# The first load of a repeat-RMSNorm kernel in two parts of 16 and 112 partitions, and gamma in one transfer

## Chip, cores and metric

The kernel runs on one core of a Trainium2 chip. The metric is device time in microseconds (us). The time of the kernel before is the median of three runs, 238.63 us (238.59 to 238.70). The profile is of one further execution, which took 238.68 us; its recorded span is 236.73 us.

## What is computed

Every row of x (8 x 512 rows of 2,048 floats) is divided by its root mean square and multiplied by gamma, and every row appears twice, one after the other, in the output of 8 x 1,024 rows.

```python
def reference(x, gamma):
    x_rep = np.repeat(x, 2, axis=1)
    rms = np.sqrt((x_rep ** 2).mean(axis=-1, keepdims=True) + 1e-6)
    return ((x_rep / rms) * gamma[None, None, :]).astype(np.float32)
```

33.5 MB are read and 67.1 MB are written, all in 32-bit floats.

## The kernel before

The 4,096 rows are cut into four tiles of 1,024 rows. In a tile each of the 128 partitions holds eight neighbouring rows: 8 x 2,048 floats, 65,536 bytes, which lie in one piece in DRAM. One load (`load`, L49 and L50) is one transfer of such a tile, 8.4 MB. Each tile becomes two stores (`store`, L52 to L55): each takes four of the eight rows per partition, every one twice, so again 65,536 bytes per partition and 8.4 MB. There are four loads and eight stores, all issued by SP on one queue.

SBUF holds one tile `y` (L46) with 24 row slots per partition, used as three regions of eight slots: `first`, `second` and `third`. The function `four` (L89) does two input tiles and is called twice (L128, L129). It loads tile n across the end of `first` and the start of `second`, and tile n + 1 into `third`, and then works in place. `squares` (L57) has ACT square each row and sum it (L63), and then take the root of the means (L67). `scale` (L70) has DVE take the reciprocal (L73) and multiply each row by it and by gamma (L75), into every second slot. `repeat` (L80, L82) copies these rows into the slots between, on ACT or on DVE. Then the store of that half tile is issued.

The order on each engine is the order of the program text (`manual_schedule`, L84). On SP that is: load 0, load 1, four stores, load 2, load 3, four stores. A transfer that waits for compute, or for a region to come free, holds up the ones behind it on SP. The loads of the second call wait for stores of the first, whose regions they use again.

`constants` (L116) is run in the first call of `four`, after load 0 is issued in the text and before load 1. Its parts lie on other engines than SP: ACT issues two transfers of 4,096 bytes, the two halves of gamma, into partition 0 (L117 to L121); POOL copies that row to all partitions (L122); DVE sets the small constant (L123); and ACT takes a root of it (L126), with which the table for the square root is loaded. The second call (L129) has no constants. Gamma on all partitions is read by every multiplication of L75. The first square of L63 waits for load 0, and so do the first multiplication of L75 and the first store.

Of the kernel before, what the change touches and what calls it, by code (L numbers as in the profile page):

```python
# [1 line left out]

# [4 lines left out]


@with_exitstack
def kernel(  # L10
    ctx: ExitStack,
    tc: tile.TileContext,
    x: bass.AP,
    gamma: bass.AP,
    out: bass.AP,
):
    nc = tc.nc
    P = nc.NUM_PARTITIONS
    f32 = mybir.dt.float32
    Act = mybir.ActivationFunctionType  # L20
    Alu = mybir.AluOpType

    B, S, D = x.shape
    Bo, So, Do = out.shape
    R = So // S
    assert R == 2 and D == Do and B == Bo and So == S * R
    eps = 1e-6
    inv_d = 1.0 / float(D)


    K = 4
    N = B * S
    ntiles = N // (P * K)
    assert N % (P * K) == 0 and ntiles == 8
    H = 2
    x_t = x.rearrange("b s d -> (b s) d").rearrange("(n p k) d -> n p k d", p=P, k=H * K)
    out_t = out.rearrange("b s d -> (b s) d").rearrange("(n p h j) d -> n h p (j d)", p=P, h=H, j=K * R)

    singles = ctx.enter_context(tc.tile_pool(name="singles", bufs=1))
    rows = ctx.enter_context(tc.tile_pool(name="rows", bufs=1))  # L40
    junk = ctx.enter_context(tc.tile_pool(name="junk", bufs=1, space=bass.MemoryType.PSUM))
    small = ctx.enter_context(tc.tile_pool(name="small", bufs=4))

    y = rows.tile([P, 3 * K * R, D], f32, name="y")  # L46
    first, second, third = 0, K * R, 2 * K * R

    def load(n, at):  # L49
        nc.sync.dma_start(out=y[:, at : at + H * K, :], in_=x_t[n])  # L50

    def store(n, h, to):  # L52
        nc.sync.dma_start(
            out=out_t[n, h], in_=y[:, to : to + K * R, :].rearrange("p j d -> p (j d)")
        )  # L55

    def squares(at, rows):  # L57

        n = len(rows)
        ss = small.tile([P, n], f32, name=f"ss{n}")  # L60
        for c, k in enumerate(rows):
            sq = junk.tile([P, D], f32, name="sq")
            nc.scalar.activation(  # L63
                out=sq[:], in_=y[:, at + k, :], func=Act.Square, accum_out=ss[:, c : c + 1]
            )
        rms = small.tile([P, n], f32, name=f"rms{n}")
        nc.scalar.activation(out=rms[:], in_=ss[:], func=Act.Sqrt, scale=inv_d, bias=eps_t[:])  # L67
        return rms

    def scale(at, to, rows, rms):  # L70
        n = len(rows)
        rstd = small.tile([P, n], f32, name=f"rstd{n}")
        nc.vector.reciprocal(out=rstd[:], in_=rms[:])  # L73
        for c, k in enumerate(rows):
            nc.vector.scalar_tensor_tensor(  # L75
                out=y[:, to + R * k, :], in0=y[:, at + k, :], scalar=rstd[:, c : c + 1],
                in1=gamma_b[:], op0=Alu.mult, op1=Alu.mult,
            )

    def repeat(to, k0, k1, copy):  # L80
        y_r = y[:, to + R * k0 : to + R * k1, :].rearrange("p (k r) d -> p k r d", r=R)
        copy(out=y_r[:, :, 1, :], in_=y_r[:, :, 0, :])  # L82

    ctx.enter_context(tc.manual_schedule())  # L84

    half = K // 2
    up, down = list(range(K)), list(range(K - 1, -1, -1))

    def four(n, constants):  # L89


        load(n, first + K)
        constants()
        load(n + 1, third)
        for rows in (up[:half], up[half:]):
            scale(first + K, first, rows, squares(first + K, rows))
        repeat(first, 0, half, nc.scalar.copy)
        repeat(first, half, K, nc.vector.tensor_copy)
        store(n, 0, first)
        scale(second, second, down, squares(second, down))  # L100
        repeat(second, half, K, nc.scalar.copy)
        repeat(second, 0, half, nc.vector.tensor_copy)
        store(n, 1, second)
        roots = [squares(third + h * K, up) for h in range(H)]
        scale(third, first, up, roots[0])
        repeat(first, 0, half, nc.scalar.copy)
        repeat(first, half, K, nc.scalar.copy)
        store(n + 1, 0, first)
        scale(third + K, third, up, roots[1])
        repeat(third, 0, K, nc.scalar.copy)  # L110
        store(n + 1, 1, third)

    gamma_b = singles.tile([P, D], f32, name="gamma_b")
    eps_t = singles.tile([P, 1], f32, name="eps_t")

    def constants():  # L116
        for c0 in (0, D // 2):  # L117
            nc.scalar.dma_start(
                out=gamma_b[0:1, c0 : c0 + D // 2],
                in_=gamma[c0 : c0 + D // 2].partition_broadcast(1),  # L120
            )  # L121
        nc.gpsimd.partition_broadcast(out_ap=gamma_b[:], in_ap=gamma_b[0:1, :])  # L122
        nc.vector.memset(eps_t, eps)  # L123

        root = singles.tile([P, 1], f32, name="root")
        nc.scalar.activation(out=root[:], in_=eps_t[:], func=Act.Sqrt)  # L126

    four(0, constants)  # L128
    four(2, lambda: None)  # L129


# [1 line left out]
_INS = ['x', 'gamma']  # L133
_OUTS = [((8, 1024, 2048), 'float32')]


# [23 lines left out]
```

## Time and profile before

| what | value |
|---|---|
| median of three runs | 238.63 us |
| profiled execution, its own time | 238.68 us |
| its span | 236.73 us |
| DVE busy | 84.4 us, 36% |
| ACT busy | 110.2 us, 47% |
| POOL busy | 2.5 us, 1% |
| squares, L63, ACT | 32 of 1,878 ns |
| multiplications, L75, DVE | 32 of 2,349 ns |
| copies, L82 | 10 on ACT, mean 4,283 ns; 4 on DVE, mean 2,293 ns |
| loads, from issue to landing | 21.9 to 40.7 us, median 39.2 |
| stores, from issue to landing | 22.1 to 32.3 us, median 24.8 |
| ACT idle before L63, for a load | 71.3 us in two stretches, the longer 51.7 |
| packets of the two gamma transfers | 4 in all, on a queue of their own |

Busy time is that of the engines that compute; an issue of a transfer isn't counted in it. SP only issues transfers. The share of DMA is the mean over the 16 DMA engines of the core. The time from issue to landing holds the time in which a transfer waits in the queue behind earlier ones.

### The profile page before, as it was taken

To read this page: it belongs to the slowest core of one execution; us is meant where nothing else is said; L and a number is where in the kernel's file an instruction comes from. 1 tells how busy PE (TensorE), PEld (TensorE's weight loads), DVE (VectorE), ACT (ScalarE), POOL (GpSimd) and SP (SyncE) were. 2 spreads that over 40 slices of the span, in tenths; PEclk is the share of its full clock that TensorE was granted. 3 is DMA by queue.
4 is the path that set the end of the run, shared out by engine and by line. 5 is a ranking of instruction groups with operands and counts; after the bars stand their busy time and mean duration, and the time that the engine had idled before them with its cause. 6 is when DMAs were issued, how large, how long until landed. Compare 5 with 4: busy or idle time off the path is not lost.

```text
span 236.7 us, 218 instructions
## 1 busy us (share of the span) xinstructions
DVE 84.4 (36%) x47; ACT 110.2 (47%) x86; POOL 2.5 (1%) x5
## 2 busy tenths in 40 slices
DVE  0000495594699400000000008929909992000000
ACT  2001989479998460000000058991999947300000
POOL 0210000000000000000000000000000000000000
DMA  9898989999898989899898989899898989899894
GB/s 355 355 532 354 532 354 487 399 443 443 365 520 354 532 354 509 377 465 421 354 532 354 532 354 520 367 399 487 354 532 354 520 365 509 376 465 421 365 520 177
DMA packets 1733, 100.68 MB, mean 425 GB/s; under 512 B 194, under 2 KB 194, under 8 KB 196
## 3 DMA queue, kind: packets, MB, share of 16 engines
q1 hardware_dynamic: 1728, 100.66, 98.5%
q10 hardware_dynamic: 4, 0.01, 0.0%
q14 instruction: 1, 0.01, 0.0%
HBM read 33.56 MB, written 67.11 MB: 425 GB/s over the span
## 4 chain that ended last, share of the span: by engine, by line
DMA 45%; ACT 26%; DVE 13%; issue 1%; DVEq 0%; SPq 0%
DMA y<-in_x_dram 26%; DMA out_dram<-y 20%; ACT sq L63 15%; DVE y L75 13%; ACT y L82 11%; ACT rms L67 1%; DVE rstd L73 0%; DVEq L75 0%; SPq L50 0%
## 5 line engine op out<-in xcount | busy, mean ns | idle before, releaser
L63 ACT ACTIVATE sq<-y 128x2048 f32<-128x2048 f32 x32 | 60.1, 1878 | 72.0 <-DMA y<-in_x_dram 71.3
L75 DVE SCALAR_TENSOR_TENSOR y<-y,rstd,gamma_b 128x2048 f32<-128x2048 f32 x32 | 73.8, 2349 | 2.1 <-DMA out_dram<-y 1.5
L82 ACT COPY y<-y 128x4096 f32<-128x4096 f32 (+1 forms) x10 | 42.6, 4283 | 19.5 <-DVE y L75 19.5
L73 DVE RECIPROCAL rstd<-rms 128x4 f32<-128x4 f32 (+1 forms) x10 | 1.7, 170 | 109.0 <-ACT rms L67 109.0
L82 DVE COPY y<-y 128x4096 f32<-128x4096 f32 x4 | 9.2, 2293 | 0.1
L63 ACT ACTIVATION_READ_ACCUMULATOR sq<-y 128x1 f32 x32 | 6.0, 186 | 0.0
L67 ACT ACTIVATE rms<-ss,eps_t 128x4 f32<-128x4 f32 (+1 forms) x10 | 3.0, 297 | 0.3
L122 POOL PARTITION_BROADCAST gamma_b<-gamma_b x1 | 2.3, 2294 | 10.2 <-DMA gamma_b<-in_gamma_dram 10.2
L126 ACT ACT_TABLE_LOAD x1 | 1.3, 1283 | 1.5 <-PEq L144 1.5
L123 DVE MEMSET eps_t<- 128x1 f32 x1 | 0.1, 59 | 0.8 <-PEq L144 0.8
L126 ACT ACTIVATE root<-eps_t 128x1 f32<-128x1 f32 x1 | 0.2, 203 | 0.0
L144 POOL MEMSET const-bfloat16-1.0<- 128x1 bf16 x1 | 0.1, 103 | 0.0
L144 POOL MEMSET const-float32-0.0<- 128x1 f32 x1 | 0.1, 100 | 0.2 <-issue 0.2
L144 POOL MEMSET const-uint8-127<- 128x1 uint8 x1 | 0.1, 102 | 0.0
L144 POOL MEMSET const-float32-1.0<- 128x1 f32 x1 | 0.1, 99 | 0.0
## 6 DMA issues: line engine op xcount, KB each, us to landing
out_dram<-y SPq DMA_DIRECT2D x8, 24.8
y<-in_x_dram SPq DMA_DIRECT2D x4, 39.2
gamma_b<-in_gamma_dram ACTq DMA_DIRECT2D x2, 4.0 KB
```

The lines of the kernel that those rows point to most:

```text
L63: nc.scalar.activation(out=sq[:], in_=y[:, at + k, :], func=Act.Square, accum_out=ss[:, c : c + 1])
L67: nc.scalar.activation(out=rms[:], in_=ss[:], func=Act.Sqrt, scale=inv_d, bias=eps_t[:])
L73: nc.vector.reciprocal(out=rstd[:], in_=rms[:])
L75: nc.vector.scalar_tensor_tensor(out=y[:, to + R * k, :], in0=y[:, at + k, :], scalar=rstd[:, c : c + 1], in1=gamma_b[:], op0=Alu.mult, op ...
L82: copy(out=y_r[:, :, 1, :], in_=y_r[:, :, 0, :])
L122: nc.gpsimd.partition_broadcast(out_ap=gamma_b[:], in_ap=gamma_b[0:1, :])
L123: nc.vector.memset(eps_t, eps)
L126: nc.scalar.activation(out=root[:], in_=eps_t[:], func=Act.Sqrt)
L144: nc = _bacc.Bacc("TRN2", target_bir_lowering=False, num_devices=1)
```

## The change

Load 0 is issued as two transfers: one of partitions 0 to 15, and one of partitions 16 to 127. The other three loads stay whole. Gamma comes in one transfer of 8,192 bytes in place of two halves. The number of transfers in the program stays 14. On ACT, DVE and POOL the order and number of computing instructions are as before; the first square on ACT waits for both parts of load 0.

```diff
+    LEAD = 16
...
-    def load(n, at):
-        nc.sync.dma_start(out=y[:, at : at + H * K, :], in_=x_t[n])
+    def load(n, at, p0=0, p1=P):
+        nc.sync.dma_start(out=y[p0:p1, at : at + H * K, :], in_=x_t[n, p0:p1])
...
-        load(n, first + K)
+        if n == 0:
+
+            load(n, first + K, 0, LEAD)
+            load(n, first + K, LEAD, P)
+        else:
+            load(n, first + K)
         constants()
         load(n + 1, third)
...
     def constants():
-        for c0 in (0, D // 2):
-            nc.scalar.dma_start(
-                out=gamma_b[0:1, c0 : c0 + D // 2],
-                in_=gamma[c0 : c0 + D // 2].partition_broadcast(1),
-            )
+        nc.scalar.dma_start(out=gamma_b[0:1, :], in_=gamma.partition_broadcast(1))
         nc.gpsimd.partition_broadcast(out_ap=gamma_b[:], in_ap=gamma_b[0:1, :])
```

## The prediction

> **What bounds the kernel now.** I read the page's slices and queue table first, then the transfer view of the first 6 us, the timeline, and last the chain of waits.
>
> ```profile
> span 236.7 us, 218 instructions
> ...
> DMA  9898989999898989899898989899898989899894
> GB/s 355 355 532 354 532 354 487 399 443 443 365 520 354 532 354 509 377 465 421 354 532 354 532 354 520 367 399 487 354 532 354 520 365 509 376 465 421 365 520 177
> ...
> q1 hardware_dynamic: 1728, 100.66, 98.5%
> ...
> HBM read 33.56 MB, written 67.11 MB: 425 GB/s over the span
> ```
>
> Columns of the queue line: packets, MB, share of the 16 DMA engines' span. The 16 engines are busy 98.5% of the span; there is no idle slice, and the mean is 425 GB/s. The trace's transfer records split the 1,728 packets into 1,536 of 65,536 bytes (one partition's eight rows of x, or of the output) and 192 of four bytes (one per engine and transfer, when it is done). So each engine carries 96 large packets, 8 per transfer in 12 transfers. The median large packet took 2.418 us, and the four-byte packets that end one transfer and the next lie 19.318 to 19.326 us apart: 8 x 2.414 and some 7 ns. 96 x 2.414 = 231.7 us of the 236.73 us span. The rest is the start (first packet at 1.73 us), a slow first packet per engine (2.4 to 3.4 us), some 0.5 to 0.7 us at 115.7 to 119 us where loads follow stores, and 1.3 us from the last packet's end (235.46) to the span's end.
>
> ```profile
> DMA  0000000000099090900900000000000999990000
> GB/s 0 0 0 0 0 0 0 0 0 0 27 2621 3058 0 437 0 437 0 0 437 0 0 0 0 0 0 0 0 0 0 0 1311 2621 1311 874 874 0 0 0 0
> ```
>
> This is 0 to 6 us in slices of 0.15 us; a packet's bytes are put where it starts. 2621 GB/s over 0.15 us is six packets, 3058 is seven, 437 is one: thirteen engines start by 1.95 us, the others at 2.18, 2.53 and 2.91 us. The second sixteen start from 4.7 us on.
>
> ```profile
> 0.72 0.76 ACTq L118 DMA_DIRECT2D gamma_b<-in_gamma_dram  x2
> 0.72 0.86 SPq L50 DMA_DIRECT2D y<-in_x_dram  x2
> ...
> 1.51 1.28 ACT L126 ACT_TABLE_LOAD   x1 [1.51 <-PEq L144]
> ...
> 10.59 2.29 POOL L122 PARTITION_BROADCAST gamma_b<-gamma_b  x1 [10.16 <-DMA gamma_b<-in_gamma_dram]
> 22.61 1.88 ACT L63 ACTIVATE sq<-y 128x2048 f32<-128x2048 f32 x1 [19.61 <-DMA y<-in_x_dram]
> ...
> 27.27 4.62 DVE L75 SCALAR_TENSOR_TENSOR y<-y,rstd,gamma_b 128x2048 f32<-128x2048 f32 x2
> ...
> 39.15 0.35 SPq L53 DMA_DIRECT2D out_dram<-y  x1
> ```
>
> Columns: start, duration, engine, line, operation. The first load's rows have landed at 22.61 us, its squares start, and the first store is issued at 39.15, while the second load's last packets run until 40.9 to 41.6. Gamma's copies land by 10.59; its first reader starts at 27.27.
>
> ```profile
> 0.72 21.87 DMA y<-in_x_dram
> ...
> 76.05 23.85 DMA out_dram<-y
> ...
> 99.98 38.68 DMA y<-in_x_dram
> ...
> 196.54 7.02 ACT y L82
> ```
>
> The chain of waits puts 26% on ACT and 13% on DVE, and ends with a copy at 196.54. It stops there because no instruction follows the last store; the 33 us after it are transfers. The stretches of ACT and DVE in it lie beside a full queue; the 38.68 us of the load at 99.98 are twice 19.3, since it waits behind a store. So the bound is packets per engine, without a gap: whatever lengthens one engine's packets moves the end one for one, and compute has room.
>
> **The change part by part.** The sum is made against the profiled execution, 238.68 us (span 236.73, 1.95 outside it); the median of the three runs is 238.63, 0.05 less.
>
> *Issues.* SP issues three loads in place of two at the start (0.34 to 0.43 us each). The second load's issue moves from 1.16 to about 1.54, and it is needed only when the first one's packets end (21.6): 20 us of cover. If that cover were gone it would cost 0.38. The stores behind it wait for compute until 39.15 anyway. Sixteen more four-byte packets, one per engine: 7 ns by the spacing above.
>
> *Gamma.* One issue on ACT in place of two (512 and 213 ns). The table load at 1.51 may come 0.2 to 0.5 earlier, ahead of an ACT that idles from 3.0 to 22.6: nothing. Before, its 4,096-byte packets took 0.156 and 0.159 us on one engine, the second only at 7.50 behind two large ones; one of 8,192 bytes takes the same 0.31. POOL's broadcast (2.29) moves from 10.59 to perhaps 3, or stays; even 14 us late it would be ready for 27.27.
>
> *Waits.* The first square on ACT, the first DVE multiply and the first store wait for both parts of the load; the part of 112 decides. One or two more semaphore steps (17 to 50 ns in the trace) lie ahead of the store at 39.15, which has about 1.8 us of queue behind it (to 41). If the load itself gets longer, the second load behind it ends later by as much, so this margin stays for the engine that is last. Engines that finish early may run dry before the store; they do not set the end.
>
> *Start.* With one packet per engine to describe, the first packet may start sooner. Bound: SP's issue ends at 1.11 and the first packet starts at 1.73, so 0 to -0.62; nothing shows that the number of packets sets this, I take 0.
>
> *The lead of 16 partitions.* It has 1 MiB: 16 packets, one per engine. [...] Not shown is whether sixteen neighbouring partitions can take sixteen packets at once. Lower end: they can, 2.418 us, +0. Upper end: one after another, 16 x 2.418 = 38.7, +36.3. Far apart; the geometric middle is four packets one after another, 4 x 2.418 = 9.67 us, **+7.25**, and I take it. It would be +0 too if only a few engines carried the lead while the others went on with the 112.
>
> [...]
>
> *The 112 partitions.* Seven packets per engine: 7 x 2.418 = 16.9 us unshared, +0. [...] Paired all the time: 33.9 us, +16.9; every step as bad as the lead: 7 x 9.67 = 67.7, +50.8. It is nearest to the 128-partition row (seven eighths of it), so I stay near the lower end and take the geometric middle of unshared and paired, 16.9 x 1.414 = 23.9, **+7.0**. The later load, on the engines that are ahead, may clash with those that are behind; I count that in this term.
>
> Sum: 238.68 + 7.25 + 7.0 = **252.9 us**.
>
> **The rivals.**
>
> (1) *Lead only.* The 112 run clean. For: they are nearly the whole width. Against: their split over the engines is new. 238.68 + 7.25 = 245.9.
>
> (2) *No sharing: not slower.* The sixteen engines write the lead at full rate, as they do at every moment of before; the count of large packets per engine stays 96. Decided at the first packet: if it ends about 3 us after its start as now, this is it. Price: 7 ns more and 0 to 0.62 less, so 238.1 to 238.7; 238.6 most likely. What else moves it is an instruction fetch: at 152.64 a packet of 8,192 bytes (0.309 us) on another queue held up one engine, which ended at 235.46 against 235.04 for the next. On another engine it could give 0.4 back, or not. For: nothing in before limits an engine but its own 27.1 GB/s. Against: that rate is the same for all engines in all 1,500 packets, and whole-width transfers alone cannot tell whether it belongs to the engine or to the place that is written.
>
> (3) *Every step shared.* If the 112 are dealt in turn, sixteen neighbours are written at each step: 9.67 + 67.7 = 77.4 in place of 19.3, so 296.7. Against: the whole load, dealt so, would be as slow, and isn't.
>
> (4) *Little sharing,* two packets one after another in the lead: +2.4, 241.1.
>
> **How the numbers follow.** Forecast (both terms) 0.46, with its own range of 248.3 (one packet of the seven paired, +2.4) to 258.0 (five paired, +12.1); lead only 0.26 (to 1 us about 245.9); no sharing 0.18; every step 0.06; little sharing 0.04. A measurement of this kernel can tell about 0.2% (0.5 us) from no change. Of the 0.18, 0.04 fall below 238.15, 0.13 within, 0.01 above. Slower: 0.46 + 0.26 + 0.06 + 0.04 + 0.01 = 0.83. Range: without every step (0.06) the top is 258.0; dropping no sharing as well would leave out over 0.2, so the low end takes it in, 238.2. That leaves out 0.06, about 0.04 at the bottom and some 0.05 of the forecast's upper tail.
>
> **What would show it.** In the changed profile: first packets of some 10 us instead of 3, so in the window of the first 6 us sixteen packets start and no second sixteen; then packets of 2.4 to 4.8 us until the load lands at about 22.6 + 14 = 37 us (30 if lead only, 22.6 if no sharing); from there the old spacing of 19.32 per transfer, every later time moved alike, and the first store some 16.5 us after the landing. Gamma's broadcast stays before the first multiply. I am wrong if the first packets stay at 3 us, if time goes missing later than the first two loads, or if the queue has idle slices.

## The result and the profile after

The changed kernel takes 261.14 us (median of five runs, 260.88 to 261.62) against 238.59 us for the kernel before on the same chip (five runs, 238.51 to 238.70). The ratio is 1.0946, with a 95% interval of 1.0935 to 1.0958: it is slower by 22.5 us, and 3.1 us above the top of the predicted range. The profiled execution has a span of 259.53 us, 22.8 more than before.

First the head of the page of the changed kernel: span, the busy share of the DMA engines and the rate in 40 slices of 6.5 us, and the DMA queue of SP (packets, MB, share).

```profile
span 259.5 us, 218 instructions
...
DMA  9879988979799799799799999898999899899794
GB/s 163 162 162 323 283 202 303 485 343 465 343 485 465 343 485 465 343 485 465 343 485 394 404 475 444 374 476 384 434 475 465 364 465 475 354 465 485 343 465 182
...
q1 hardware_dynamic: 1744, 100.66, 98.0%
```

Compare the row of the DMA engines' busy share (DMA, in tenths) with the row of the rate (GB/s). The engines count as busy all along, 98.0% against 98.5% before, and yet in the first seven slices (45 us) they move 162 to 323 GB/s, and in the later ones, but for the last, 343 to 485. Busy time alone doesn't show this loss: the packets are in flight all the time, only each takes longer.

The transfer view of the first 6 us (slices of 0.15 us, as it was shown of before):

```profile
DMA  0000000000199900990000000000000000000000
GB/s 0 0 0 0 0 0 0 0 0 0 55 1748 2621 1748 0 0 437 437 0 0 0 0 0 0 0 0 0 0 0 0 0 0 0 0 0 0 0 0 0 0
```

Sixteen packets start, between 1.74 and 2.61 us, and then none: before, the second sixteen had started by 5.4 us. Both rows count a packet in the slice in which it starts, so a 0 says that no packet started there, not that the engines stood still: by the transfer records these sixteen ran until 9.3 to 11.4 us. The timeline (start, duration, engine, line, operation) has what follows:

```profile
0.73 1.39 SPq L51 DMA_DIRECT2D y<-in_x_dram  x3
...
2.62 2.29 POOL L124 PARTITION_BROADCAST gamma_b<-gamma_b  x1 [2.19 <-DMA gamma_b<-in_gamma_dram]
44.56 1.88 ACT L64 ACTIVATE sq<-y 128x2048 f32<-128x2048 f32 x1 [41.78 <-DMA y<-in_x_dram]
...
61.08 0.37 SPq L54 DMA_DIRECT2D out_dram<-y  x1
```

Load 0 lands for the first square at 44.56 us (before 22.61), and the first store is issued at 61.08 (before 39.15): 16.5 us behind the landing in both. Everything after the first load is moved by 22 us and else as it was. Gamma's broadcast starts at 2.62 us in place of 10.59, and nothing gains by it.

The trace's transfer records give the packets of load 0. A round is here sixteen packets, one per engine. The medians of the eight rounds in us:

| | 1 | 2 | 3 | 4 | 5 | 6 | 7 | 8 | sum |
|---|---|---|---|---|---|---|---|---|---|
| before | 3.04 | 2.42 | 2.42 | 2.42 | 2.42 | 2.42 | 2.42 | 2.42 | 20.0 |
| after: lead, then the 112 | 8.73 | 5.41 | 4.74 | 2.90 | 3.74 | 4.48 | 4.61 | 4.41 | 39.0 |

The median engine loses 19.0 us here. Two engines lose some 2 us more: in the fourth round, where the others' packets took 2.8 to 3.2 us, theirs took 4.6 and 4.7, and their last ones took 4.8 against 4.3 to 4.7. The last four-byte packet of load 0 is at 43.52 us against 22.23 before, 21.3 us later, and the last packet of the kernel ends at 258.22 us against 235.47, 22.75 us later. Of the 1.5 us between these two, 0.4 appear in load 1, whose first packets took 2.8 to 3.4 us, and the rest where load 2 follows stores; why it appears there is open.

### The profile page after: what moved, and what is told of

It is laid out like the page before. It is cut to its first block, busy times and chain, and to the rows that moved or that the text cites. A ratio compares the mean times of both kernels' runs of the same rounds, so it can differ in the third digit from the quotient of the medians.

```text
span 259.5 us, 218 instructions
## 1 busy us (share of the span) xinstructions
DVE 84.4 (33%) x47; ACT 110.2 (42%) x86; POOL 2.5 (1%) x5
## 4 chain that ended last, share of the span: by engine, by line
DMA 50%; ACT 24%; DVE 12%; issue 1%; SPq 0%; DVEq 0%; ACTq 0%
DMA y<-in_x_dram 32%; DMA out_dram<-y 18%; ACT sq L64 14%; DVE y L76 12%; ACT y L83 10%; ACT rms L68 0%; DVE rstd L74 0%; SPq L51 0%; DVEq L76 0%; ACTq L64 0%
```

## The experiments

Eight kernels were run. The theory at the outset ("place"): packets slow each other when the sixteen engines write partitions that lie close together or otherwise share something in SBUF. Its rivals: "source" (reading neighbouring blocks of DRAM at one time is slow), "shape" (any transfer that hasn't 128 partitions is slow), and that the two transfers as such, or gamma, are dear.

**Gamma alone.** The kernel before, with the edit of gamma only:

```diff
-        for c0 in (0, D // 2):
-            nc.scalar.dma_start(
...
+        nc.scalar.dma_start(out=gamma_b[0:1, :], in_=gamma.partition_broadcast(1))
```

> The kernel before with gamma in one transfer, load 0 whole. Every theory that puts the loss on the split load: no change, 238.3 to 238.9 us, with POOL's broadcast of gamma starting at about 2.6 us as in the changed kernel. If gamma's transfer were the cause: some 261 us.

Measured: 238.80 us against 238.74, ratio 1.000 (0.9991 to 1.0009). The broadcast of gamma comes 8 us sooner and the first square, which waits for load 0, does not:

```profile
2.62 2.29 POOL L118 PARTITION_BROADCAST gamma_b<-gamma_b  x1 [2.19 <-DMA gamma_b<-in_gamma_dram]
22.53 1.88 ACT L63 ACTIVATE sq<-y 128x2048 f32<-128x2048 f32 x1 [19.77 <-DMA y<-in_x_dram]
```

Gamma's part of the change is worth nothing.

**The split alone.** The changed kernel with gamma in two halves, so that only the split of load 0 is left of the change.

> The changed kernel with gamma in two halves again. If the split of load 0 is the whole cause: 261 us (260.5 to 261.8), the first sixteen packets taking 8 to 9.3 us as in the changed kernel. If the loss needs the gamma packet on a lead engine: back near 238.6.

Measured: 261.12 us (one run). The whole loss is that of the split load. Gamma's second half now arrives late, its broadcast starts at 12.96 us, and the first multiplication doesn't need it before 48.

**Two halves of 64 partitions.**

```diff
-    LEAD = 16
+    LEAD = 64
```

> Load 0 in two halves of 64 partitions, gamma in one transfer. Place theory (packets that go to partitions close together slow each other; the lead's 8.7 us against 2.42 is 3.6 times): in each half sixteen engines share half of the width, so a packet takes about twice 2.42, the load 8 x 4.84 = 38.7 in place of 19.3, in all about 258 us. Source theory (sixteen packets that read neighbouring 64 KB blocks of DRAM at one time slow each other): engines read blocks four apart, as far as in the whole load if each engine takes neighbours, so about 239 us. Shape theory (any transfer that hasn't 128 partitions is slow, like the 112 at 30 us in place of 16.9, 1.8 times): 8 x 2.42 x 1.8 = 34.8, about 254 us.

Measured: 260.76 us (one run), above the 258 of the place theory and far from the 239 of the source theory. The records show why it is more: after the first round, packets take 4.92 to 5.14 us, not 4.84, and the medians of the eight rounds of load 0 add up to 40.4 us in place of the 20.0 before. Shape isn't excluded by this run, which missed all three numbers.

**The same first load split by rows, not by partitions.** Both transfers have all 128 partitions: one row of 8 KB of each, then seven.

```diff
-        nc.sync.dma_start(out=y[p0:p1, at : at + H * K, :], in_=x_t[n, p0:p1])
+        nc.sync.dma_start(out=y[:, at + k0 : at + k1, :], in_=x_t[n, :, k0:k1])
...
-            load(n, first + K, 0, LEAD)
-            load(n, first + K, LEAD, P)
+            load(n, first + K, 0, 1)
+            load(n, first + K, 1, H * K)
```

> Load 0 in two transfers again, but both over all 128 partitions: the first of the eight rows of each partition, then the other seven; gamma in one transfer. Place and shape theory: every transfer has the whole width, so no loss: 238.3 to 239.2 us. Source theory: packets of 8 and 56 KB from the same spacing as the whole load, also no loss. If two transfers in place of one are dear as such: clearly slower, towards 261.

Measured: 239.42 us, ratio 1.0035 (1.0022 to 1.0047). Two transfers in place of one are not what costs 22 us. It is 0.2 us over what I expected. Load 0's last packet is no later than before (22.20 us), load 1's is by 1.0 us, with packets of 3.3 to 3.9 us near 38.6; why these are slow was not pursued.

**Loads by themselves.** This kernel computes no norm and stores only two pieces at the end; each load waits until the one before has landed and DVE has marked the tile. The lines that load (blocks are the 64 KB pieces of x, one per partition):

```
L42  y[:]         <- blocks[0:128]          L54  y[64:80]    <- blocks[192:208]
L44  y[:]         <- blocks[128:256]        L56  y[0:32]     <- blocks[224:256]
L46  y[0:16]      <- blocks[0:16]           L58  y[0:64]     <- blocks[256:320]
L48  y[0:16]      <- blocks[0:512:32]       L60  y[16:128]   <- blocks[320:432]
L50  y[0:128:8]   <- blocks[128:144]        L62  y[0:112]    <- blocks[384:496]
L52  y[0:112:7]   <- blocks[160:176]        L64, L66: one row, seven rows of all
```

> Only loads, one after another, each alone on the queue (DVE marks the tile between them); no norm is computed and only two small stores are made, so its time is not to be compared. Per packet of 64 KB: whole load of 128 partitions 2.42 us (all theories), about 21.9 us from issue to landing. Sixteen partitions 0 to 15 from sixteen neighbouring blocks of DRAM: 8 to 9.3 us as in the changed kernel. The same partitions from blocks 2 MB apart: place theory 8 to 10 us again; source theory near 2.5 to 3. Partitions 0, 8, ... 120 or 0, 7, ... 105 from neighbouring blocks: place theory 2.4 to 5 us; source theory 8 to 9.3. Partitions 64 to 79: as 0 to 15 by place and source theory. 32 partitions: place theory about half of the lead's slowing, some 10 us for two packets per engine. 64 partitions: place theory 19 to 20 us for four packets, source theory about 10. 112 partitions, 16 to 127 and 0 to 111: between 17 (no slowing when alone) and 30 us (slow by itself); shape theory 30 for both. One row of 8 KB per partition over 128 partitions: about 4 us; seven rows: 17 to 19.

The timeline of the marks (L39): the idle time in brackets is DVE's wait for the load that was issued just before it, in the order of the lines above, from L42 to L62.

```profile
23.02 0.07 DVE L39 MEMSET y<- 128x8 f32 x1 [22.14 <-DMA y<-in_x_dram]
45.07 0.07 DVE L39 MEMSET y<- 128x8 f32 x1 [21.99 <-DMA y<-in_x_dram]
56.90 0.07 DVE L39 MEMSET y<- 128x8 f32 x1 [11.77 <-DMA y<-in_x_dram]
69.12 0.07 DVE L39 MEMSET y<- 128x8 f32 x1 [12.15 <-DMA y<-in_x_dram]
76.86 0.07 DVE L39 MEMSET y<- 128x8 f32 x1 [7.67 <-DMA y<-in_x_dram]
84.28 0.07 DVE L39 MEMSET y<- 128x8 f32 x1 [7.36 <-DMA y<-in_x_dram]
96.13 0.07 DVE L39 MEMSET y<- 128x8 f32 x1 [11.79 <-DMA y<-in_x_dram]
108.51 0.07 DVE L39 MEMSET y<- 128x8 f32 x1 [12.31 <-DMA y<-in_x_dram]
131.55 0.07 DVE L39 MEMSET y<- 128x8 f32 x1 [22.98 <-DMA y<-in_x_dram]
166.00 0.07 DVE L39 MEMSET y<- 128x8 f32 x1 [34.39 <-DMA y<-in_x_dram]
198.89 0.07 DVE L39 MEMSET y<- 128x8 f32 x1 [32.83 <-DMA y<-in_x_dram]
```

The third and fourth waits are one and the same load of partitions 0 to 15, from neighbouring blocks (11.77 us) and from blocks 2 MB apart (12.15); their packets take 8.1 to 9.3 and 7.7 to 9.2 us. So it isn't the source. Sixteen partitions spread out (7.67 and 7.36 us) are faster than sixteen neighbours with the same bytes, so it isn't the number of partitions. 32 neighbours take hardly longer than 16 (12.31), and 64 take 22.98, as long as all 128 (22.14). Partitions 64 to 79 take 11.79, like 0 to 15. And the 112 partitions take 34.39 us (16 to 127) and 32.83 us (0 to 111) alone: seven packets per engine, longer than the eight of the whole load, and longer than the 30 that I had put as the upper end. Their seven rounds have medians of 4.3, 4.8, 3.5, 3.9, 4.4, 4.8 and 4.5 us in the one, and of 4.6, 4.8, 4.8, 3.3, 3.3, 4.6 and 4.8 in the other. So the slow 112 of the changed kernel need no lead ahead of them. One thing remained open: the set seven apart was expected between 2.4 and 5 us per packet, and none of its packets came near 2.4; all took 3.8 to 5.2.

**Places.** Only small transfers, without a norm, each once. Six of them have the same form and the same kind of source and differ in the first partition alone (L42 to L52).

```
L42  y[32:96:4]    L48  y[20:84:4]     L54  y[11:117:7]   L60  y[0:4]      L66  y[0:128:64]
L44  y[36:100:4]   L50  y[48:112:4]    L56  y[0:1]        L62  y[0:8:4]    L68 to L72  stores of
L46  y[40:104:4]   L52  y[0:64:4]      L58  y[0:2]        L64  y[0:64:32]  0:16, 32:96:4, 40:104:4
```

> Only small transfers, each alone; no norm is computed, and only three pieces of the output are stored, so its time is not to be compared. Sixteen partitions four apart, with the same sixteen neighbouring packets of DRAM each, and only the first partition moved: 32 to 92, 36 to 96, 40 to 100, 20 to 80, 48 to 108, 0 to 60. Source and shape theory: all of these alike, since source and shape are the same. Place theory: they differ; the fastest takes some 3 us per packet (2.42 and the 0.6 of a first packet), the slowest as long as 32 or 64 neighbours did, 4.6 to 5.1. [...] Stores of 0 to 15: 10 us per packet as in the earlier run; of 32 to 92 four apart: about 3.

The waits of the marks, again in the order of the lines, L42 to L72:

```profile
23.25 0.07 DVE L39 MEMSET y<- 128x8 f32 x1 [5.32 <-DMA y<-in_x_dram]
30.32 0.07 DVE L39 MEMSET y<- 128x8 f32 x1 [7.01 <-DMA y<-in_x_dram]
37.74 0.07 DVE L39 MEMSET y<- 128x8 f32 x1 [7.35 <-DMA y<-in_x_dram]
45.20 0.07 DVE L39 MEMSET y<- 128x8 f32 x1 [7.40 <-DMA y<-in_x_dram]
52.90 0.07 DVE L39 MEMSET y<- 128x8 f32 x1 [7.64 <-DMA y<-in_x_dram]
60.45 0.07 DVE L39 MEMSET y<- 128x8 f32 x1 [7.48 <-DMA y<-in_x_dram]
65.59 0.07 DVE L39 MEMSET y<- 128x8 f32 x1 [5.08 <-DMA y<-in_x_dram]
70.29 0.07 DVE L39 MEMSET y<- 128x8 f32 x1 [4.63 <-DMA y<-in_x_dram]
76.70 0.07 DVE L39 MEMSET y<- 128x8 f32 x1 [6.35 <-DMA y<-in_x_dram]
87.81 0.07 DVE L39 MEMSET y<- 128x8 f32 x1 [11.04 <-DMA y<-in_x_dram]
92.97 0.07 DVE L39 MEMSET y<- 128x8 f32 x1 [5.11 <-DMA y<-in_x_dram]
99.82 0.07 DVE L39 MEMSET y<- 128x8 f32 x1 [6.78 <-DMA y<-in_x_dram]
104.94 0.07 DVE L39 MEMSET y<- 128x8 f32 x1 [5.06 <-DMA y<-in_x_dram]
116.68 0.07 DVE L39 MEMSET y<- 128x8 f32 x1 [11.68 <-DMA out_dram<-y]
121.07 0.07 DVE L39 MEMSET y<- 128x8 f32 x1 [4.32 <-DMA out_dram<-y]
127.91 0.07 DVE L39 MEMSET y<- 128x8 f32 x1 [6.77 <-DMA out_dram<-y]
```

The first six alone settle it. Partitions 32 to 92 land after 5.32 us, and moving the set by four partitions makes that 7.01; moving it by eight 7.35, and then it hardly grows. The set seven apart that begins at partition 11 takes 5.08. Shape and source are the same in the six, so only the place is left. The sets of two say which partitions slow each other: 0 and 1, and 0 and 32, are slow (6.35 and 6.78 us), 0 and 4, and 0 and 64, are nearly as fast as one partition (5.11 and 5.06 against 4.63), and four neighbours take 11.04. In packets, partition 0 alone took 3.3 us, 0 and 1 took 4.2 to 4.4, and 0 to 3 took 7.7 to 8.7. Other sets of two were not tried.

The transfer records show the packets one by one. Beside each set of sixteen stands how many of its partitions are new, that is, not in the first set (32, 36, ... 92):

| set | new | packets, us |
|---|---|---|
| load, 32 to 92 | 0 | 2.4 to 3.1 |
| load, 36 to 96 | 1 | two of 4.1, the others 2.5 to 3.2 |
| load, 40 to 100 | 2 | all 4.2 to 5.2 |
| load, 20 to 80 | 3 | all 4.4 to 5.2 |
| load, 48 to 108 | 4 | all 3.9 to 4.9 |
| load, 0 to 60 | 8 | all 4.2 to 5.1 |
| store, 32 to 92 | 0 | 2.45 |
| store, 40 to 100 | 2 | four of 4.7, twelve of 2.5 |
| store, 0 to 15 | 16 | 9.8 to 10.2 |

So in the sets four apart two of a load's sixteen packets are slow with one new partition (4.1 us), and all sixteen from two on (3.9 to 5.2); in a store with two only four are (4.7). The number alone decides nothing: of the set seven apart from 11 thirteen are new, and it landed after 5.08 us. How the 112 partitions are dealt to the engines stands in no trace, and no more does it for the 128 of a whole load, whose packets took 2.42 us. In each of the four short rounds of the two 112 loads (third and fourth of the one, fourth and fifth of the other) exactly two packets are long: 4.8 and 4.9, then 4.4 and 4.6 us in the one, 4.8 and 4.8, then 4.3 and 4.5 in the other, where the remaining fourteen took 2.9 to 3.9. In the changed kernel, too, exactly two packets are long in the fourth and fifth rounds of load 0, 4.6 and 4.7, then 4.4 and 4.4 us; the first two are those of the engines that come last. That looks like the set with one new partition, only that the fourteen are slower than its 2.5 to 3.2, which isn't explained. In the other five rounds of the changed kernel's 112 all sixteen packets took 4.1 to 6.0 us, like the sets with two and more. It is no more than a likeness: which partitions meet in a round was not shown.

**The cost inside the whole kernel.** The kernel with gamma in one transfer and load 0 whole gets an extra load of 0.5 MB ahead of it, which nobody uses: half packets for sixteen neighbours, or for sixteen partitions four apart.

```diff
+        if n == 0:
+            nc.sync.dma_start(out=y[0:16, first : first + K, :], in_=x_t[3, 0:16, 0:K])
         load(n, first + K)
```

> The kernel before with gamma in one transfer, load 0 whole, and ahead of it one more load that nobody uses: half a packet (32 KB) to each of the partitions 0 to 15. If the lead costs what it does because of where it writes, in the whole kernel as alone: half of 8.7 us, so 4.4 more: 242.6 to 243.6. If a short transfer at the head is what costs, this and the next kernel are alike.

> The same with the 16 half packets going to partitions 32, 36, ... 92. Place theory: 32 KB on each engine at 2.42 us for 64 KB, 1.2 more: 239.7 to 240.4. Source and shape theory: as e5, 242.6 to 243.6.

Measured: near 242.83 us, ratio 1.0176 (1.0161 to 1.0191); far, with `y[32:96:4]` there, 240.59 us, 1.0081 (1.0065 to 1.0098). The issues of the two (kernels near, then far; last number: us from issue to landing):

```profile
y<-in_x_dram SPq DMA_DIRECT2D x1, 512.0 KB, 7.4
```

```profile
y<-in_x_dram SPq DMA_DIRECT2D x1, 512.0 KB, 3.8
```

The same bytes in the same form cost 4.1 us near and 1.85 far over the kernel before, whose runs beside them had a median of 238.74. The near one is as expected, the far one 0.2 us above the expected range; its packets themselves took 1.3 to 2.1 us. The place theory holds in the whole kernel, and source and shape fall.

No run points to a version faster than the kernel before. That kernel has the 16 engines busy for 98.5% of its span, at the whole-width rate of 2.418 us a packet, the fastest steady rate that any 64 KB packet had here.

## Why the prediction was wrong

**What bounds the kernel** was read rightly: the engines' packets. A loss in the first load went through to the end, and compute and the waits on semaphores hid nothing of it: the first store still follows the landing by 16.5 us. One of the signs of being wrong did show in small: 1.1 us went missing later than the first two loads, and no run tells why.

**Issues, gamma, waits, start**: each at nothing, and nothing it was. Gamma alone gave a ratio of 1.000. The three loads were issued within 1.39 us from 0.73. The first packets start from 1.74 to 2.61 us in place of 1.73 to 2.91: a smaller first transfer starts no sooner. That engines which are ahead may run dry before the first store without setting the end, came true for fourteen of them: their load 1 ended between 60.8 and 61.5 us, and their first store packets start from 61.9 on.

**The lead**: put at 9.67 us and +7.25. Its packets took 8.73 us in the median. The second round starts at 10.67 us in the median, against 4.93 before, so it cost +5.7. That sixteen neighbours are slowed was right, and the size 1.5 too large: 0.9 because a packet took 8.73 and not 9.67, and 0.6 because I compared it with a steady packet of 2.418, where a first one takes 3.04 anyway. That it came so near was partly luck: four packets one after another was the middle between two far ends, not read from a row. The same 1 MiB by itself took 9.40 us from its first packet's start to its last one's end, 112 GB/s.

**The 112 partitions** are the step that failed: "It is nearest to the 128-partition row (seven eighths of it), so I stay near the lower end and take the geometric middle of unshared and paired, 16.9 x 1.414 = 23.9, +7.0." Measured were 30.3 us in the median engine (the sum of its seven rounds) against 16.9, +13.4: five rounds of 4.4 to 5.4 us (+11.6) and the other two at 2.9 and 3.7 (+1.8). The last two engines lost some 2.2 more. With the 1.5 us after load 0, 5.7 + 13.4 + 2.2 + 1.5 makes 22.8, the difference of the two spans. The row was chosen by the number of partitions, but that number says nothing about it: 16 partitions took 5.3 us or 7.4 us by the place of the first one alone. No run shows the pairing of two engines from which the +7.0 was taken; in its place the records show five rounds of seven in which all sixteen packets were slow, and two in which two took 4.4 to 4.7 us and the rest 2.8 to 3.8. And in the set with two new partitions not four packets were slow but all sixteen (4.2 to 5.2 us), which no row of before could have shown. The case that I wrote down as an end, all seven paired, gave +16.9 and 262.8 us, and is nearer to the measured 261.1 than the value that I took. My range closed at "five paired", +12.1, which left out that the other two rounds lengthen too, the engines that come last, and the 1.5 us after load 0. The clash with the later load, which the prediction counted in this term, was there and small: the 0.4 us in load 1.

**The rivals.** Lead only (245.9) fell, since the 112 are slow alone. No sharing (238.6) fell at the first packet, where it was to be decided: 8.7 us, not 3, so that an engine's 27.1 GB/s (65,536 bytes in 2.418 us) became 7.5. Little sharing (241.1) fell with the lead's 8.7 us, which is more than two packets one after another. Every step as bad as the lead (296.7) fell too: the rounds of the 112 took 2.9 to 5.4 us, not 9.67. The other signs given in advance were right: no second sixteen within 6 us, the later times moved alike; the first square was to start at 37 us, and started at 44.6.

## What to carry to other kernels

Where DMA is the bound, leave a load whole over the 128 partitions; to cut it, cut along the rows of each partition, which cost 0.35% here (one row, then seven) where the cut by partitions cost 9.5%. A transfer over a part of the partitions has to be judged by where its packets go at one moment, not by its bytes or by how many partitions it has: 64 neighbours took as long as all 128 (22.98 us against 22.14), and 112 took half as long again (34.39 and 32.83). Sixteen took 5.1 to 12.2. Look at the rate and at the duration of single packets: the busy share of the DMA engines read 98% in both kernels.

## What was not expected of the hardware

Two partitions in other places slowed a whole load of sixteen. With one new partition, two packets took 4.1 us and the others 2.5 to 3.2; with two, all sixteen took 4.2 to 5.2, as with eight (4.2 to 5.1). A store with two had only four slow packets: 4.7 us, and 2.5 for the other twelve. The cause of this difference wasn't tried. From partitions 0 to 15 a store's packets took 10.0 us, into them a load's 8.7; that is 4.1 and 3.6 times 2.418.
